# A hybrid conv/gMLP trunk: group A's LayerNorm placed between output products, four convolution operations per projection tile, late page splits, 1/rms chains on GpSimd

## The chip, the cores and the metric

One Trainium2 chip, one of its cores. The metric is the device time of one execution in microseconds (us); lower is better. The kernel before takes 972.72 us (median of 3 runs, 972.19 to 973.91). The engines are TensorE (PE; its weight loads are listed apart as PEld), VectorE (DVE), ScalarE (ACT), GpSimd (POOL) and SyncE (SP), which issues the DMAs here.

## The reference

There are two layers over 256 tokens of width 1024, in float32. Each layer is a half SwiGLU (1024 to 2816 to 1024), a mixer, and a second half SwiGLU; an RMSNorm stands ahead of each, and one at the end.

```
h = rms_norm(x, mix_norm[l]);  p = h @ w_in[l]        # split into A, B, C
a = silu(layer_norm(conv31(a_val * sigmoid(a_gate)) + conv_a_b))      # group A, 384 channels
b = gelu(b_u) * (tril(w_s) applied to layer_norm(gelu(b_v)) + b_s)    # group B, 256 channels
c = c_b * conv3(c_c * c_x)                                            # group C, 384 channels
x = x + concat(a, b, c) @ w_out[l]
x = x + 0.5 * (silu(h @ w_gate) * (h @ w_up)) @ w_down                # each half SwiGLU
```

## The kernel before

Activations lie with channels on partitions (128 x 256 tiles), except the residual `x_sb`, which lies with tokens on partitions in four banks (`c`: half of the tokens, `h`: half of the channels). Weights come as a stream of 128 x 1024 pages in the order of use, through 5 raw buffers (`load_to`, L137), loaded by the SP queue. Most pages are split into a rounded part `hi` (ACT, L151) and a rest `lo` (DVE, L152), so that TensorE can work with fast float32r products: `mm_wide` (L186) takes two, `mm_three` and `mm_out` (L202) three matmuls per block. The three `w_out` pages of group A are used unsplit (`native`, L155), by slow float32 matmuls (L206). `split_to` (L144) splits ahead of use, up to `AHEAD` pages and never beyond `state["cap"]`. Each `lo` is ordered behind the last operation of the latest 1/sqrt chain that the program had written before it (`held[0]`, set in `rsqrt`, L287).

The compiler's scheduler orders each engine's instructions: the earlier a statement stands in the program, the higher its priority, and an instruction that is not ready is passed by later ones. On the chip each engine then runs its list in order. `pin` (L97) fixes an instruction behind the one that the program wrote before it on the same engine. `mm_wide`, `mm_native`, transposes, sums and rows are pinned; `mm_three` and `mm_out` are not.

A half SwiGLU (`ffn`, L414) goes over 22 tiles f: gate and up products, an evacuation through DVE and ACT into the split `m2`, and the down products of tile f - 2 into four PSUM banks. The last three tiles' down products are taken bank by bank (`bank`), each bank is added to `x_sb`, squared and summed, and `Norm.turn` transposes it for the next stage, a bank later (`drain_banks`, L398). `Norm.rstd` then makes 1/rms by a chain of 12 small DVE operations (`rsqrt`, L270). `Norm.lead` (L384) starts the next stage: the first half (4 of 8 blocks) of three tiles, then the second halves; the matmuls that spread 1/rms over the partitions (`rows`, L375, `pb`, L299) stand behind the first tile's second half.

The very first norm has nothing before it: the first two pages are used natively, then `sums` (L343) squares the input, adds it up, and sums over channels on TensorE, with a 1/sqrt chain on DVE, and only then comes the first split page.

The mixer (`mixer`, L568) projects 19 tiles by `mm_three`. Three of them are made in `lead`; each of the 16 others draws `BACK` = 3 operations from the list of convolution steps of group A (`conv_ops`, L539): 21 per channel tile and 63 in all, each four ACT products with one DVE addition, or one DVE multiply-add, or one of two closing sums. 48 are drawn so; the remaining 15 follow after group B and C. Then `layer_norm` (L516) of group A is written: mean over channels on TensorE (L521), centring on DVE (L525), squares on ACT (L527), sums on TensorE (L309), the 1/sqrt chain on DVE, a row on TensorE (L299), scaling on DVE (L722), Silu on ACT (L724). The 20 output products of groups B and C (5 pages, 4 banks, 60 matmuls) are written behind it but are unpinned, so they run ahead of it. The 12 native output products of group A close the stage bank by bank.

Of the kernel before, what the change touches and what calls it, by code (L numbers as in the profile page):

```python
# [59 lines left out]
PARTS = 15  # L60
LOAD_AHEAD = 5
AHEAD = 11
PACE = 1.6
NEXT = 5
WORK = 12
# [3 lines left out]
LAST = 3  # L69
STEPS = 3  # L70
AFTER = 2
WIDE = 16
BACK = 3
# [3 lines left out]
def hybrid_trunk(ctx, tc, x_t, x_n, par, gain, w_st, b_s, wts, out):  # L77
# [124 lines left out]
    def mm_out(ps, x2, page, c, h, first, last):  # L202

        t, n = slice(c * P, (c + 1) * P), slice(h * N, (h + 1) * N)
        if len(x2.shape) == 2:
            nc.tensor.matmul(ps, x2[:, t], page[:, n], start=first, stop=last)  # L206
            return
        xh, xl = x2[:, 0, t], x2[:, 1, t]
        wh, wl = (p[:, n] for p in page)
        nc.tensor.matmul(ps, xh, wh, start=first, stop=False)  # L210
        nc.tensor.matmul(ps, xh, wl, start=False, stop=False)  # L211
        nc.tensor.matmul(ps, xl, wh, start=False, stop=last)  # L212
# [57 lines left out]
    def rsqrt(ss, scale, eps, name, n=TC):  # L270
# [5 lines left out]
        nc.vector.tensor_scalar(m, ss, scale, eps, ALU.mult, ALU.add)  # L276
        yi = t("i", dtype=I32)
        nc.vector.tensor_scalar(yi, m.bitcast(I32), -0.5, RSQRT_SEED, ALU.mult, ALU.add)
# [3 lines left out]
        nc.vector.tensor_mul(g, m, y)  # L282
        for it in range(3):
            r = t("r")
            y2 = t("y") if it < 2 else t("out", 4)
            nc.vector.scalar_tensor_tensor(r, g, -0.5, y, ALU.mult, ALU.mult)
            held[0] = nc.vector.scalar_tensor_tensor(y2, r, 1.5, y, ALU.add, ALU.mult)  # L287
            if it < 2:
                g2 = t("g")
                nc.vector.scalar_tensor_tensor(g2, r, 1.5, g, ALU.add, ALU.mult)  # L290
                g = g2
            y = y2
# [22 lines left out]
    class Norm:  # L315
# [54 lines left out]
        def rstd(self):  # L370
            s = tmp.tile([P, TC], F32, tag="rs_s", name=f"{self.id}_s")
            nc.vector.tensor_add(s, self.ss[:, :, 0], self.ss[:, :, 1])
            self.rs = rsqrt(s, 1.0 / D, RMS_EPS, self.id)
# [10 lines left out]
        def lead(self, tiles, want):  # L384

            ks = range(DT // 2), range(DT // 2, DT)
            got = None
            for mm, ps, w in tiles:
                mm(ps, w, self.act, ks[0])
                while self.later:  # L390
                    self.later.pop(0)()
            for mm, ps, w in tiles:
                mm(ps, w, self.act, ks[1])
                if got is None:
                    got = self.rows(want)
# [18 lines left out]
    def ffn(l, s, norm, nxt):  # L414
# [5 lines left out]
        if norm.first:  # L420
# [7 lines left out]
            norm.sums()  # L428
# [3 lines left out]
            rb, = norm.rows([AF.Copy])  # L432
# [7 lines left out]
        mm_wide(tiles[1][1], w1[1], act, range(DT))  # L440
        rh = tmp.tile([P, TC], F32, tag="rh", name=f"{nm}_rh")
# [74 lines left out]
    def layer_norm(tiles, eps, name, between=None, more=1):  # L516
# [13 lines left out]
        if between is not None:  # L530
            for _ in range(STEPS):
                between()
        y = rsqrt(token_sums(sq, name), 1.0 / (n * P), eps, name)
        if between is not None:
            for _ in range(more):
                between()
        return xc, row(y, name)
# [30 lines left out]
    def mixer(l, norm, nxt):  # L568
# [9 lines left out]
        state["cap"] = state["at"] + NIN + NB + NC  # L578
# [92 lines left out]
        xc, pr = layer_norm(vs, LN_EPS, f"{nm}_lv", step, AFTER)  # L671
# [43 lines left out]
        for k in range(NA, DT):  # L715
            split_mix(k)
        drain(len(back))
        use([MM], [MM, SM])
        xc, pr = layer_norm(conv, LN_EPS, f"{nm}_la")
        for i in range(NA):  # L720
# [5 lines left out]

        po = {b: ps_d.tile([P, N], F32, tag=f"d{b[0]}{b[1]}", name=f"{nm}_po{b[0]}{b[1]}")
              for b in banks}
        first, last = OUT_ORDER[0], OUT_ORDER[-1]
# [5 lines left out]
        state["cap"] = None  # L735
# [88 lines left out]
```

## Time and profile before

| | |
|---|---|
| median of 3 runs | 972.72 us |
| the profiled execution's own time | 972.09 us |
| its span, first to last instruction | 970.4 us |
| PE busy | 941.5 us (97%) |
| DVE busy | 703.9 us (73%) |
| ACT busy | 534.7 us (55%) |
| POOL busy | 2.3 us, 14 instructions |
| granted TensorE clock, mean | 0.987 |

Times inside the trace count from the start of the span. The granted clock has two levels, 2.4 GHz (1.00) and 1.2 GHz; a mean between them is a mixture over the stretch. TensorE is busy nearly all the time, so what can be won lies in its idle stretches and in the parts that ran at the lower clock.

### The profile page before, as it was taken

Reading aid. Unit: us, or ns where it says so; the run is one execution under the profiler, and the core shown is the slowest. Engines: PE = TensorE matmul, PEld = TensorE weight load, DVE = VectorE, ACT = ScalarE, POOL = GpSimd, SP = SyncE. Lnnn points to the kernel's source line nnn. Section 1 sums busy time; section 2 is a strip of 40 time slices with the busy share of each in tenths; the row PEclk is TensorE's granted clock in tenths of the full one; section 3 lists DMA queues with packets and bytes.
Section 4 is the critical chain, followed back from the end, with each engine's and each line's share of the span. In section 5 each row is a group of like instructions: output and inputs, shape, how many; then the busy total and the mean of one; then the engine's idle time right before and its main releaser. Section 6 shows DMA issues by size and latency. Waiting matters only on the chain.

```text
span 970.4 us, 13953 instructions
## 1 busy us (share of the span) xinstructions
PE 941.5 (97%) x5192; PEld 803.7 (83%) x5192; DVE 703.9 (73%) x1202; ACT 534.7 (55%) x906; POOL 2.3 (0%) x14
## 2 busy tenths in 40 slices
PE   7999999999989999999999999999999799999996
PEld 6888888889957888888878888888998488888884
DVE  5986666679978966666696666666898698666634
ACT  4865455468446755545565455455863576455512
POOL 0000000000000000000000000000000000000000
PEclk9999999999989999999999999999999799999999
DMA  8895555525117965555455555553430488555301
GB/s 290 314 321 192 184 195 185 185 88 174 61 43 239 328 213 194 187 185 193 153 191 183 191 195 183 187 194 111 157 127 1 136 293 290 193 195 192 113 1 43
DMA packets 48451, 172.22 MB, mean 177 GB/s; under 512 B 5376, under 2 KB 5760, under 8 KB 48384
## 3 DMA queue, kind: packets, MB, share of 16 engines
q1 hardware_dynamic: 48384, 171.34, 50.6%
q8 instruction: 40, 0.66, 0.3%
q14 instruction: 27, 0.22, 0.1%
HBM read 170.27 MB, written 1.05 MB: 177 GB/s over the span
## 4 chain that ended last, share of the span: by engine, by line
PE 88%; DVE 5%; DMA 3%; ACT 2%; issue 1%; SPq 0%; DVEq 0%; ACTq 0%
PE f_pu L191 15%; PE f_pg L191 15%; PE f_pd L210 8%; PE f_pd L211 8%; PE f_pd L212 8%; PE f_pu L192 8%; PE f_pg L192 8%; PE m_p L199 4%; PE m_p L200 4%; PE m_p L198 4%; DMA raw<-wts 3%; PE m_po L206 2%; DVE lo L152 1%; PE m_po L210 1%; PE m_po L211 1%
## 5 line engine op out<-in xcount | busy, mean ns | idle before, releaser
L152 DVE TENSOR_TENSOR lo<-raw,hi 128x1024 fp32r<-128x1024 f32 x310 | 377.2, 1223 | 185.2 <-ACT hi L151 168.3
L151 ACT CAST hi<-raw 128x1024 fp32r<-128x1024 f32 x310 | 323.8, 1049 | 258.3 <-PE f_pg L191 88.8
L191 PE MATMUL f_pg<-ffn_norm_x,hi 128*128 128x512 f32 x696 | 250.8, 400 | 1.4 <-DVE ffn_norm_x L368 1.4
L191 PE MATMUL f_pu<-ffn_norm_x,hi 128*128 128x512 f32 x696 | 250.8, 400 | 0.0
L192 PE MATMUL f_pg<-ffn_norm_x,lo 128*128 128x256 f32 x696 | 195.9, 281 | 0.0
L192 PE MATMUL f_pu<-ffn_norm_x,lo 128*128 128x256 f32 x696 | 195.4, 281 | 0.0
L191 PEld LDWEIGHTS f_pg<-ffn_norm_x,hi 128*128 128x128 f32 x696 | 131.5, 189 | 34.0 <-DVE ffn_norm_x L368 2.6
L191 PEld LDWEIGHTS f_pu<-ffn_norm_x,hi 128*128 128x128 f32 x696 | 130.8, 188 | 32.2
L210 PE MATMUL f_pd<-hi,f_m 128*128 128x512 f32 x352 | 138.9, 395 | 2.2 <-DVE f_wu_sm L221 2.2
L211 PE MATMUL f_pd<-lo,f_m 128*128 128x512 f32 x352 | 138.3, 393 | 0.0
L212 PE MATMUL f_pd<-hi,f_m 128*128 128x512 f32 x352 | 136.5, 390 | 0.0
L192 PEld LDWEIGHTS f_pg<-ffn_norm_x,lo 128*128 128x128 f32 x696 | 132.0, 190 | 3.0
L192 PEld LDWEIGHTS f_pu<-ffn_norm_x,lo 128*128 128x128 f32 x696 | 131.6, 189 | 0.0
L199 PE MATMUL m_p<-mix_norm_x,hi 128*128 128x256 f32 x304 | 86.8, 287 | 0.8 <-DVE mix_norm_x L368 0.8
L200 PE MATMUL m_p<-mix_norm_x,lo 128*128 128x256 f32 x304 | 85.9, 284 | 0.0
L198 PE MATMUL m_p<-mix_norm_x,hi 128*128 128x256 f32 x304 | 85.0, 286 | 0.0
L210 PEld LDWEIGHTS f_pd<-hi,f_m 128*128 128x128 f32 x352 | 66.1, 188 | 19.4 <-DVE f_wu_sm L221 3.4
L212 PEld LDWEIGHTS f_pd<-hi,f_m 128*128 128x128 f32 x352 | 66.0, 188 | 14.9 <-DVE f_m L467 0.7
L211 PEld LDWEIGHTS f_pd<-lo,f_m 128*128 128x128 f32 x352 | 66.1, 188 | 10.4
L199 PEld LDWEIGHTS m_p<-mix_norm_x,hi 128*128 128x128 f32 x304 | 58.2, 191 | 1.8 <-DVE mix_norm_x L368 1.2
L200 PEld LDWEIGHTS m_p<-mix_norm_x,lo 128*128 128x128 f32 x304 | 58.2, 192 | 0.2 <-issue 0.2
L198 PEld LDWEIGHTS m_p<-mix_norm_x,hi 128*128 128x128 f32 x304 | 57.3, 191 | 0.2 <-issue 0.2
(230 smaller groups left out, 821.5 us busy)
## 6 DMA issues: line engine op xcount, KB each, us to landing
raw<-wts SPq DMA_DIRECT2D x316, 512.0 KB, 4.3
xt<-x_t SPq DMA_DIRECT2D x4, 256.0 KB, 5.4
raw<-wts SPq DMA_DIRECT2D x4, 256.0 KB, 5.6
x_sb<-x_n SPq DMA_DIRECT2D x2, 512.0 KB, 7.2
out<-y SPq DMA_DIRECT2D x4, 256.0 KB, 2.2
wst<-w_st SPq DMA_DIRECT2D x2, 256.0 KB, 3.7
gfin<-gain SPq DMA_DIRECT2D x1, 512.0 KB, 5.6
bsb<-b_s SPq DMA_DIRECT2D x2, 128.0 KB, 3.8
```

The lines of the kernel that those rows point to most:

```text
L151: nc.scalar.copy(hi, loaded[i])
L152: after(nc.vector.tensor_sub(lo, loaded[i], hi), held[0])
L191: pin(nc.tensor.matmul(ps, wh, x2, start=k == 0, stop=False))
L192: pin(nc.tensor.matmul(ps[:, 0, :], wl, x2[:, 0, :], start=False, stop=k == DT - 1))
L198: nc.tensor.matmul(ps, wh, x2[:, 0, :], start=k == 0, stop=False)
L199: nc.tensor.matmul(ps, wh, x2[:, 1, :], start=False, stop=False)
L200: nc.tensor.matmul(ps, wl, x2[:, 0, :], start=False, stop=k == DT - 1)
L206: nc.tensor.matmul(ps, x2[:, t], page[:, n], start=first, stop=last)
L210: nc.tensor.matmul(ps, xh, wh, start=first, stop=False)
L211: nc.tensor.matmul(ps, xh, wl, start=False, stop=False)
L212: nc.tensor.matmul(ps, xl, wh, start=False, stop=last)
```

## The change

It pins the output products and writes group A's LayerNorm as a generator, resumed after the 6th, 11th and 16th of the 20 output products. `BACK` rises to 4, so that all 63 convolution steps are drawn with the projections. The cap on page splits falls by the three `w_out` pages of group C, which are split just ahead of their products. `Norm.rstd` moves to GpSimd (15 operations in place of 12). `lead` writes `rows` ahead of all second halves. In the first SwiGLU the first split page's gate product stands ahead of `sums`, and `rows` behind the up product. Sizes change with it.

```diff
-PARTS = 15
+PARTS = 16
-AHEAD = 11
+AHEAD = 13
-NEXT = 5
-WORK = 12
+NEXT = 4
+WORK = 10
+CHAIN = (5, 10, 15)
-BACK = 3
+BACK = 4
...
     def mm_out(ps, x2, page, c, h, first, last):
...
-            nc.tensor.matmul(ps, x2[:, t], page[:, n], start=first, stop=last)
+            pin(nc.tensor.matmul(ps, x2[:, t], page[:, n], start=first, stop=last))
...
-        nc.tensor.matmul(ps, xh, wh, start=first, stop=False)
-        nc.tensor.matmul(ps, xh, wl, start=False, stop=False)
-        nc.tensor.matmul(ps, xl, wh, start=False, stop=last)
+        pin(nc.tensor.matmul(ps, xh, wh, start=first, stop=False))
+        pin(nc.tensor.matmul(ps, xh, wl, start=False, stop=False))
+        pin(nc.tensor.matmul(ps, xl, wh, start=False, stop=last))
...
-    def rsqrt(ss, scale, eps, name, n=TC):
+    def rsqrt(ss, scale, eps, name, n=TC, eng=None):
+        v = nc.vector if eng is None else eng
...
-            nc.vector.scalar_tensor_tensor(r, g, -0.5, y, ALU.mult, ALU.mult)
-            held[0] = nc.vector.scalar_tensor_tensor(y2, r, 1.5, y, ALU.add, ALU.mult)
+            if eng is None:
+                v.scalar_tensor_tensor(r, g, -0.5, y, ALU.mult, ALU.mult)
+                held[0] = v.scalar_tensor_tensor(y2, r, 1.5, y, ALU.add, ALU.mult)
+            else:
+                v.tensor_mul(r, g, y)
+                v.tensor_scalar(r, r, -0.5, 1.5, ALU.mult, ALU.add)
+                v.tensor_mul(y2, r, y)
             if it < 2:
                 g2 = t("g")
-                nc.vector.scalar_tensor_tensor(g2, r, 1.5, g, ALU.add, ALU.mult)
+                if eng is None:
+                    v.scalar_tensor_tensor(g2, r, 1.5, g, ALU.add, ALU.mult)
+                else:
+                    v.tensor_mul(g2, r, g)
...
         def rstd(self):
-            nc.vector.tensor_add(s, self.ss[:, :, 0], self.ss[:, :, 1])
-            self.rs = rsqrt(s, 1.0 / D, RMS_EPS, self.id)
+            nc.gpsimd.tensor_add(s, self.ss[:, :, 0], self.ss[:, :, 1])
+            self.rs = rsqrt(s, 1.0 / D, RMS_EPS, self.id, eng=nc.gpsimd)
...
         def lead(self, tiles, want):
...
+            got = self.rows(want)
             for mm, ps, w in tiles:
                 mm(ps, w, self.act, ks[1])
-                if got is None:
-                    got = self.rows(want)
...
     def ffn(l, s, norm, nxt):
...
             split_to(4)
-            norm.sums()
             tiles[1] = [psum(wide, f"{nm}_1_pg")]
             w1 = weights(2, False)
             mm_wide(tiles[1][0], w1[0], act, range(DT))
-            rb, = norm.rows([AF.Copy])
+            norm.sums()
...
         mm_wide(tiles[1][1], w1[1], act, range(DT))
+        if norm.first:
+            rb, = norm.rows([AF.Copy])
...
     def mixer(l, norm, nxt):
...
-        state["cap"] = state["at"] + NIN + NB + NC
+        state["cap"] = state["at"] + NIN + NB
...
-        for k in range(NA, DT):
+        drain(len(back))
+        state["cap"] = None
+        use([MM], [MM, SM])
...
+        ln = layer_norm(conv, LN_EPS, f"{nm}_la")
+        xc = None
+        for n, k in enumerate(OUT_ORDER[:DT - NA]):
             split_mix(k)
-        drain(len(back))
-        use([MM], [MM, SM])
-        xc, pr = layer_norm(conv, LN_EPS, f"{nm}_la")
+            w = weights(1, False)[0]
+            for i, (c, h) in enumerate(banks):
+                mm_out(po[c, h], mix[k], w, c, h, k == first, k == last)
+                if n * len(banks) + i in CHAIN:
+                    xc = next(ln)
+        xc, pr = xc
...
-        for k in OUT_ORDER[:DT - NA]:
-            w = weights(1, False)[0]
-            for c, h in banks:
-                mm_out(po[c, h], mix[k], w, c, h, k == first, k == last)
```

The generator `layer_norm` stops three times: after mean, centring and squares; after sums and the 1/sqrt chain (on DVE, as before); after the row.

## Rows read from the trace of the kernel before

**Rows 1.** Waits of PE over the whole span: total us, times, longest.

```profile
PE m_po L206 <- ACT m_ay L724: 2.5, 1, 2.5
...
PE f_pg L191 <- DVE ffn_norm_x L368: 1.4, 2, 1.0
```

**Rows 2.** Stretches: length, busy time (count) per engine, clock, DMA share, GB/s.

```profile
264.05:299.32 35.27, 31.61 (x117) 20.83 (x116) 26.42 (x56) 17.35 (x31) 0.64 (x1) 0.90 0.23 81
737.12:773.64 36.52, 31.56 (x117) 21.00 (x115) 25.90 (x56) 17.61 (x33) 0.00 (x0) 0.86 0.20 68
...
218.00:264.00 46.00, 45.92 (x384) 44.97 (x383) 43.86 (x90) 30.98 (x62) 0.00 (x0) 1.00 0.34 115
```

**Rows 3.** Timeline of PE, first mixer's output stage: start, duration, instruction, wait before it.

```profile
277.18 0.39 PE L210 MATMUL m_po<-hi,m_mix 128*128 128x512 f32 x1
...
277.86 0.39 PE L210 MATMUL m_po<-hi,m_mix 128*128 128x512 f32 x1
...
283.71 1.23 PE L299 MATMUL m_la_pb<-ident,m_la_out 128*128 128x128 f32 x4 [1.96 <-DVE m_la_out L287]
286.08 7.37 PE L206 MATMUL m_po<-raw,m_ao 128*128 128x512 f32 x12 [1.15 <-ACT m_ao L724]
293.29 0.60 PE L362 MATMUL ffn_norm_pt<-ident,x_sb 128*128 128x128 f32 x4
293.72 2.74 PE L206 MATMUL m_po<-raw,m_ao 128*128 128x512 f32 x6
```

**Rows 4.** Timelines of ACT and DVE there: a page's hi, the 1/sqrt chain, its lo.

```profile
272.55 1.03 ACT L151 CAST hi<-raw 128x1024 fp32r<-128x1024 f32 x1
...
281.78 0.16 DVE L276 TENSOR_SCALAR m_la_m<-m_la_ps 128x2 f32<-128x2 f32 x1 [1.67 <-PE m_la_ps L309]
...
283.57 1.23 DVE L152 TENSOR_TENSOR lo<-raw,hi 128x1024 fp32r<-128x1024 f32 x1
```

**Rows 5.** Groups of DVE, 264.05 to 279.45, then 210 to 264.05: busy, mean ns.

```profile
L563 DVE SCALAR_TENSOR_TENSOR m_ac_acc<-apad,par_sb,m_ac_acc 128x256 f32<-128x256 f32 x10 | 4.3, 478 | 0.1
L556 DVE TENSOR_TENSOR m_ac_acc<-m_ac_acc,m_ac_t 128x1024 f32<-128x1024 f32 x2 | 2.5, 1226 | 1.3 <-ACT m_ac_t L554 1.2
...
L152 DVE TENSOR_TENSOR lo<-raw,hi 128x1024 fp32r<-128x1024 f32 x12 | 14.4, 1216 | 0.5 <-ACT hi L151 0.5
```

**Rows 6.** Timeline of PE around the first norm.

```profile
19.28 0.58 PE L309 MATMUL ffn_norm_ps<-ones,ffn_norm_sq 128*128 128x1 f32 x4 [3.88 <-DVE ffn_norm_sq L351]
...
24.52 0.48 PE L191 MATMUL f_pu<-ffn_norm_x,hi 128*128 128x512 f32 x1
...
27.38 0.39 PE L191 MATMUL f_pg<-ffn_norm_x,hi 128*128 128x512 f32 x1
```

**Rows 7.** Timeline of PE at the end of the first and the last SwiGLU.

```profile
193.49 0.40 PE L210 MATMUL f_pd<-hi,f_m 128*128 128x512 f32 x1
...
196.69 0.42 PE L210 MATMUL f_pd<-hi,f_m 128*128 128x512 f32 x1
...
952.56 0.40 PE L210 MATMUL f_pd<-hi,f_m 128*128 128x512 f32 x1
...
954.60 0.50 PE L210 MATMUL f_pd<-hi,f_m 128*128 128x512 f32 x1
```

**Rows 8.** Timelines: POOL's rows, DVE beside one, ACT and PE after the first mixer.

```profile
1.10 0.17 POOL L253 MEMSET zpad<- 128x2 f32 x3
1.29 0.29 POOL masks.py:199 TENSOR_SCALAR_AFFINE_SELECT ident<-ident 128x128 f32<-128x128 f32 x1
72.47 0.74 POOL L260 TENSOR_SCALAR_AFFINE_SELECT wst<-wst 128x512 f32<-128x512 f32 x1 [70.88 <-DMA wst<-w_st]
...
72.64 0.85 DVE L467 TENSOR_TENSOR f_m<-f_m,f_m 128x256 fp32r<-128x256 f32 x1
...
300.94 0.19 ACT L356 ACTIVATION_READ_ACCUMULATOR ffn_norm_sq<-x_sb 128x1 f32 x1
...
303.12 0.40 PE L191 MATMUL f_pg<-ffn_norm_x,hi 128*128 128x512 f32 x1
```

More of the change, by code (lines that the diff above doesn't have):

```diff
@@ L275, in rsqrt @@
         m = t("m")
-        nc.vector.tensor_scalar(m, ss, scale, eps, ALU.mult, ALU.add)
+        v.tensor_scalar(m, ss, scale, eps, ALU.mult, ALU.add)
         yi = t("i", dtype=I32)
-        nc.vector.tensor_scalar(yi, m.bitcast(I32), -0.5, RSQRT_SEED, ALU.mult, ALU.add)
+        v.tensor_scalar(yi, m.bitcast(I32), -0.5, RSQRT_SEED, ALU.mult, ALU.add)
         y = yi.bitcast(F32)
         g = t("g")
-        nc.vector.tensor_mul(g, m, y)
+        v.tensor_mul(g, m, y)
         for it in range(3):
@@ L386, in lead @@
             ks = range(DT // 2), range(DT // 2, DT)
-            got = None
             for mm, ps, w in tiles:
@@ L513, in finish, with layer_norm @@
                 nc.sync.dma_start(out[c, :, h * N:(h + 1) * N], y)
-    def layer_norm(tiles, eps, name, between=None, more=1):
+    def layer_norm(tiles, eps, name, eng=None):
         n = len(tiles)
@@ L529, in layer_norm @@
             sq.append(q)
[L530 to L537, printed above, removed]
+        yield
+        y = rsqrt(token_sums(sq, name), 1.0 / (n * P), eps, name, eng=eng)
+        yield
+        yield xc, row(y, name)
     def conv_ops(l, i, ap, out, name):
@@ L670, in mixer @@
         step()
-        xc, pr = layer_norm(vs, LN_EPS, f"{nm}_lv", step, AFTER)
+        ln = layer_norm(vs, LN_EPS, f"{nm}_lv")
+        for n in (STEPS, AFTER):
+            next(ln)
+            for _ in range(n):
+                step()
+        xc, pr = next(ln)
         vn = []
@@ L712, in mixer @@
             pass
-        for k in range(NA, DT):
-            split_mix(k)
-        drain(len(back))
-        use([MM], [MM, SM])
-        xc, pr = layer_norm(conv, LN_EPS, f"{nm}_la")
+        drain(len(back))
+        state["cap"] = None
+        use([MM], [MM, SM])
+        po = {b: ps_d.tile([P, N], F32, tag=f"d{b[0]}{b[1]}", name=f"{nm}_po{b[0]}{b[1]}")
+              for b in banks}
+        first, last = OUT_ORDER[0], OUT_ORDER[-1]
+        ln = layer_norm(conv, LN_EPS, f"{nm}_la")
+        xc = None
+        for n, k in enumerate(OUT_ORDER[:DT - NA]):
+            split_mix(k)
+            w = weights(1, False)[0]
[4 more added lines that the diff above has]
+        xc, pr = xc
         for i in range(NA):
@@ L725, in mixer @@
             mix[i] = a
-        po = {b: ps_d.tile([P, N], F32, tag=f"d{b[0]}{b[1]}", name=f"{nm}_po{b[0]}{b[1]}")
-              for b in banks}
-        first, last = OUT_ORDER[0], OUT_ORDER[-1]
-        for k in OUT_ORDER[:DT - NA]:
-            w = weights(1, False)[0]
-            for c, h in banks:
-                mm_out(po[c, h], mix[k], w, c, h, k == first, k == last)
         wn = dict(zip(OUT_ORDER[DT - NA:], native(NA)))
-        state["cap"] = None
         split_to(state["at"] + NEXT)
```

## The prediction

> **What bounds the kernel.** The table of busy times gives TensorE 97% of the span, so the next question is where its remaining idle time lies. The list of its waits names the stages: group A's LayerNorm at the end of each mixer, and the evacuation of the transposed residual ahead of a SwiGLU [rows 1]. In the view by stretches, the output stage of the two mixers lasts 35.27 and 36.52 us with 31.61 and 31.56 us busy, at a mean clock of 0.90 and 0.86, while in the projections ahead of it TensorE leaves nothing idle and VectorE is busy 43.86 of 46.00 us [rows 2]. So the output stages lose time twice, by idling and at the lower clock, and the projection stage has hardly any VectorE time to give.
>
> The timeline of the first output stage shows how. The 60 matmuls of groups B and C run at 0.68 us a product (277.18 to 277.86). Then TensorE waits for one link of LayerNorm after another, and the clock falls: the row's four records take 1.23 us against 0.60 for four such records later, and the first 12 native records take 7.37 us where 6 take 2.74, thus 1.89 too long [rows 3]. Idle 3.66, native 1.89 and row 0.63 make 6.2 us in layer 0; idle 4.96 and the same clock losses make 7.5 in layer 1. The ceiling of this part is 13.7 us.
>
> **The change part by part**, in us against the profiled execution's 972.09; the median of the runs shown is 972.72, so 0.6 is added at the end.
>
> *LayerNorm between products.* The mean follows product 6, the sums product 11, the row product 16, and 4 products (2.7) cover scaling and Silu. That hides the chain if convolution is finished by product 6, and gives up to -13.7. Two new waits come in its place.
>
> First, the splits on use. Before, a page's hi stood ready from 272.55 + 1.03 on, but its lo ran only at 283.57, straight behind the chain that began at 281.78: each lo is ordered behind the latest chain written before it [rows 4]. In the changed program the first C page is split before the chain is written, the second and third behind it. Count from the first product: 11 products are 7.5, the mean inside them about 1, the sums about 1.2 (estimates from the records' starts), the chain 1.8 [rows 4], the lo 1.2, in all 12.7 to 12.9; the 13th product is reached at 10.4, can run its first matmul, and waits for lo: about 2.4 per mixer. It is nothing if the sums come early, and at most the chain and the lo, 3.0. I take 2.4, as both of its links stand in rows.
>
> Second, convolution moves into the projections. 10 multiply-adds (4.3) and 2 additions (2.5) ran behind 264.05, besides the closing sums [rows 5]; they now stand ahead of the output products' operands on VectorE. Against that, three lo leave the projections (3 x 1.22 [rows 5]), PARTS and AHEAD let about one more be made earlier (1.2), and 2.1 were idle [rows 2]: 6.8 + 1.1 for the closing sums - 7.0 is about 1 us by which the first product starts late. Pinning matters here: the products can no longer go out of order around a missing rest of an operand. Bounds: 0, when all of the slack is usable, and 5, when neither the idle time nor the earlier page helps; I take 1, from the balance. The scalar work on ACT has 15 us free in the same stretch [rows 2] and costs nothing; if ACT were late, the additions behind it would be. The three loads are the same, only their raw buffers are held longer, and the SP queue then brings the next stage's pages later; the 12 native products (about 11 us) cover that, and if not, the next SwiGLU would wait for a page.
>
> Sum for both mixers: -13.7 + 2 x (2.4 + 1.0) = -6.9.
>
> *First norm.* TensorE waited 3.88 us until 19.28 for the squares, then ran the gate product at the lower clock until the row; the up product began at 24.52, the next tile at 27.38, so a page's product is 2.86 at full clock [rows 6]. Now the gate product fills the hole from 15.4 to 18.2, the sums come at 19.28 as before, the up product runs until 22.6, and the row behind it finds its chain done. The next tile needs a PSUM buffer that VectorE frees some 1.5 us after the row: 24.5 instead of 27.38, **-2.9**. Bounds: -4 if that buffer is free at once, -1 if VectorE's page splits stand ahead of it.
>
> *Pinned products at the ends of the SwiGLUs.* At present 14 matmuls of other banks (193.49 to 196.69) fill the time until the last tile's operand is there; at the last SwiGLU it is there after 2.04 (952.56 to 954.60) [rows 7]. Pinned, the first bank offers 6 matmuls, 1.36 us, as filler. So 0.7 to 1.8 are lost at three ends and 0.6 at the fourth; with 1.2, in all +4.2. The first banks are then done earlier relative to the rest, so the waits for the transposed residual (1.4 [rows 1]) should go: **+2.8**, between +0.7 and +6.
>
> *Chains on GpSimd.* At five stage changes the chain becomes 15 dependent GpSimd operations, and the row, pinned, now stands ahead of all second halves. Time allowed in the one after the first mixer: the squares are there at 301.13, the third first half begins at 303.12 and takes 1.4, so 3.4 us [rows 8]. No such operation is in the trace: fills of 128x2 take 0.17 for three, the select of 128x128 takes 0.29, one of 128x512 takes 0.74 [rows 8]; VectorE's 11-step chain takes 1.8 [rows 4]. Bounds per step are 0.06 and 0.74, so 1 to 11 us per chain; I take 0.20, between the nearest rows, so 3.0. One thing speaks for more: while GpSimd ran its select, a VectorE subtraction that takes 0.42 elsewhere took 0.85 [rows 8], so the two hold each other up. One operation of 0.7 in the way makes 3.7, which is 0.3 late, with the hand-overs 0.4; five times: **+2.0**, bounds 0 and +38. If TensorE comes late here, tile evacuations wait for the row too.
>
> By itself, what a page says of this: the Trainium skill, "SBUF — State Buffer", section "SBUF: two separate sides", has VectorE and GpSimd share one port pair as an exclusive lock, held for a whole instruction, also against VectorE operations with two SBUF inputs. The subtraction above agrees. By that rule every lo that falls into a chain adds its whole length to it, which is the first rival's mechanism.
>
> *Sizes.* WORK falls to 10 and NEXT to 4; four pages are what the next stage's lead uses, and no row shows a wait for a work buffer: 0, and the next stage's splits would be late if it is short.
>
> Sum: -6.9 - 2.9 + 2.8 + 2.0 = -5.0, so 967.1 in a profiled execution and **967.7** as a median.
>
> **The rivals.** *GpSimd chains decide* (slower). Place: the row ahead of the second halves, five times. If VectorE's operations with two inputs stand in the chain's way, say two of 0.7 and two lo of 1.2 (3.8), a chain takes 6.8, TensorE is 3.4 late each time, 17 in all instead of 2: 967.7 + 15 = **982.7**. It decides when a chain is 1.4 late, that is from 4.8 us on, as all other parts are worth 7.0. For it: the stretched subtraction, and that splits are no longer ordered behind these chains, so they may fall into them. Against: in the mixers' lead the scheduler can pass the row with unpinned matmuls.
>
> *VectorE bounds the projections* (no change). If the output products start 4 late instead of 1, the mixers give -0.9 and the total is +1.0: **973.7**. For it: 43.86 of 46.00 busy. Against: the moved splits free as much as convolution adds.
>
> *Clean overlap.* Neither new wait nor late chains: -13.7 - 2.9 + 2.8 = -13.8, so **958.9**.
>
> That the change doesn't do what it says has no place of its own: if convolution ends after product 6, the fixed places turn into waits, which is the second rival.
>
> **How the numbers follow.** Forecast 0.44, clean overlap 0.20, GpSimd 0.20, VectorE 0.16. A difference of 0.2%, 1.9 us, is about what a measurement of this kernel can tell from none. Faster: clean 0.20, forecast 0.38 (its bounds reach past 970.8 for the rest), VectorE 0.02, so 0.60. Same: VectorE 0.12, forecast 0.05, GpSimd 0.03, so 0.20. Slower: 0.20. The range runs from the clean case to where most of the GpSimd case is left out: 958 to 979.
>
> **What would show it.** In the changed profile the waits of TensorE for m_la_out and m_ay should be gone, the native records should take 2.74 for 6 from the start, and a wait for lo of about 2.4 should stand before the 13th product. The wait for the first squares should be near 1 us, and a wait for the split m2 should stand at each SwiGLU's end. POOL should have 75 operations more, with each row waiting for them by under 1 us. Waits of several us for the GpSimd result, or output products starting 4 us behind the last projection, would make the prediction wrong.

## The result and the profile after

The changed kernel takes 1016.82 us (median of 4 runs, 1013.92 to 1025.95) against 972.46 (971.61 to 973.91) for the kernel before: 1.0471 times, with an interval of 1.0403 to 1.0538. The prediction was 967.7, faster. The changed kernel's four runs spread over 12 us, the slowest at the lowest mean clock (0.961) and the fastest at the highest (0.977), where the kernel before spreads over 2.3; the profiled run, used in this section, is the slowest of them.

From the page of the changed kernel: the table of busy times and TensorE's rows of the 40 slices.

```profile
span 1024.2 us, 14005 instructions
PE 964.9 (94%) x5192; PEld 823.6 (80%) x5192; DVE 695.1 (68%) x1142; ACT 532.1 (52%) x906; POOL 21.1 (2%) x89
...
PE   7899999989897999999989999999898989999996
...
PEclk9899999989978999999989999999898989999999
```

Apart from GpSimd (21.1 us, 2.3 before) no other engine is fuller than before: VectorE is at 695.1 us (703.9 before). TensorE's idle time is 59.3 us (1024.2 - 964.9) against 28.9 before, 30.4 more. Its busy time is 23.4 more (964.9 - 941.5) for the same arithmetic. So more than two fifths of the loss is matmuls that take longer. The slices show where: apart from the two ends of the run, both rows fall to 8 or 7 around the stage changes and stay at 9 between them.

TensorE's waits over the whole span (us in total, times, longest) answer to [rows 1]:

```profile
PE ffn_norm_pb L310 <- POOL ffn_norm_out L295: 9.3, 3, 3.4
PE f_pd L211 <- ACT f_m L476: 6.9, 4, 2.1
PE mix_norm_pb L310 <- POOL mix_norm_out L295: 6.5, 2, 3.3
PE m_po L211 <- DVE m_co L667: 4.8, 1, 4.8
PE f_pg L192 <- DVE ffn_norm_x L379: 4.4, 5, 1.0
PE m_po L211 <- DVE m_cv L667: 4.3, 1, 4.3
PE m_po L212 <- DVE lo L153: 4.1, 2, 2.1
PE f_pd L211 <- DVE f_wu_sm L222: 3.3, 1, 3.3
PE f_pg L192 <- DVE f_g L470: 2.4, 1, 2.4
...
PE ffn_norm_ps L320 <- DVE ffn_norm_sq L362: 0.9, 1, 0.9
```

The waits for group A's LayerNorm are gone, as intended, and the wait for the first squares fell from 3.9 to 0.9. In their place stand stops of 2 to 5 us at fourteen places (of the rows above: five for the GpSimd result, three of four for f_m, two each for the first output product and lo, one each for f_wu_sm and f_g). What a stop does to the matmuls behind it is seen in TensorE's timeline of the changed kernel, at the end of the first SwiGLU and in the first output stage [rows 3, 7]:

```profile
197.96 0.39 PE L213 MATMUL f_pd<-hi,f_m 128*128 128x512 f32 x1
200.47 0.50 PE L211 MATMUL f_pd<-hi,f_m 128*128 128x512 f32 x1 [2.13 <-ACT f_m L476]
...
276.93 0.28 PE L201 MATMUL m_p<-mix_norm_x,lo 128*128 128x256 f32 x1
281.99 0.77 PE L211 MATMUL m_po<-hi,m_mix 128*128 128x512 f32 x1 [4.79 <-DVE m_co L667]
282.56 0.63 PE L212 MATMUL m_po<-lo,m_mix 128*128 128x512 f32 x1
...
287.13 0.39 PE L212 MATMUL m_po<-lo,m_mix 128*128 128x512 f32 x1
...
297.52 0.80 PE L212 MATMUL m_po<-lo,m_mix 128*128 128x512 f32 x1 [2.05 <-DVE lo L153]
```

A record that takes 0.39 ahead of a stop takes 0.63 behind it, until some 4 to 5 us later. The view by stretches gives the clock of three of these, behind the stop at the SwiGLU's end, the one for the first output product and the one for the first mixer's row (length, busy and count of PE, PEld, DVE, ACT, POOL, then clock, DMA share, GB/s):

```profile
200.47:204.93 4.46, 4.46 (x13) 3.38 (x14) 1.16 (x2) 0.72 (x2) 0.00 (x0) 0.62 0.29 103
281.99:288.28 6.29, 6.29 (x18) 4.97 (x19) 1.66 (x3) 0.00 (x0) 0.00 (x0) 0.65 0.25 86
219.40:222.00 2.60, 2.60 (x12) 2.60 (x13) 0.00 (x0) 1.32 (x3) 0.00 (x0) 0.50 0.00 0
```

0.50 is the level of 1.2 GHz throughout. The prediction counted the new stops at their length alone.

The GpSimd chain of the first mixer's lead, from the timeline of POOL (first and last row of the chain's 15, the stretched one and the row ahead of it):

```profile
214.36 0.19 POOL L383 TENSOR_TENSOR mix_norm_s<-mix_norm_ss 128x2 f32<-128x2 f32 x1 [131.72 <-ACT mix_norm_sq L367]
...
214.92 0.19 POOL L281 TENSOR_SCALAR mix_norm_i<-mix_norm_m 128x2 int32<-128x2 int32 x1
215.19 1.04 POOL L285 TENSOR_TENSOR mix_norm_g<-mix_norm_m,mix_norm_i 128x2 f32<-128x2 f32 x1
...
219.15 0.20 POOL L295 TENSOR_TENSOR mix_norm_out<-mix_norm_r,mix_norm_y 128x2 f32<-128x2 f32 x1
```

One operation takes 0.19, and one that needs its result starts 0.28 behind it. The fourth took 1.04, beside a page's rest on VectorE that ran from 214.96 for 1.22. The whole chain takes 4.99; the other four take 4.23, 5.00, 4.99 and 4.68, each with a stretched operation in it.

The time that TensorE can bridge is the other half of such a wait. After the first mixer, in order of time: the last page's rest on VectorE ahead of the chain's start, ACT's last square, TensorE's last record ahead of the row, and the row.

```profile
322.11 1.23 DVE L153 TENSOR_TENSOR lo<-raw,hi 128x1024 fp32r<-128x1024 f32 x1
...
322.51 0.19 ACT L367 ACTIVATION_READ_ACCUMULATOR ffn_norm_sq<-x_sb 128x1 f32 x1
...
323.35 0.28 PE L193 MATMUL f_pg<-ffn_norm_x,lo 128*128 128x256 f32 x1
327.06 0.94 PE L310 MATMUL ffn_norm_pb<-ident,ffn_norm_out 128*128 128x128 f32 x4 [3.43 <-POOL ffn_norm_out L295]
```

From the squares on, which are there at 322.70, TensorE has 0.9 us of work left, until 323.63; the prediction allowed 3.4. The chain starts at 322.78, 11.3 us behind the start of the second of the four additions into the residual (311.46). In the kernel before that was 7.7 (293.49 to 301.16), with one page's rest in between; here there are four.

### The profile page after: what moved, and what is told of

The parts are those of the page before. It is cut to its first block, busy times and chain, and to the rows that moved or that the text cites. A ratio compares the mean times of both kernels' runs of the same rounds, so it can differ in the third digit from the quotient of the medians.

```text
span 1024.2 us, 14005 instructions
## 1 busy us (share of the span) xinstructions
PE 964.9 (94%) x5192; PEld 823.6 (80%) x5192; DVE 695.1 (68%) x1142; ACT 532.1 (52%) x906; POOL 21.1 (2%) x89
## 4 chain that ended last, share of the span: by engine, by line
PE 75%; issue 16%; DVE 3%; DMA 2%; POOL 2%; ACT 2%; SPq 0%; POOLq 0%; DVEq 0%; ACTq 0%
PE f_pu L192 16%; PE f_pg L192 15%; PE f_pd L211 8%; PE f_pu L193 8%; PE f_pg L193 8%; PE f_pd L212 8%; PE f_pd L213 8%; DMA raw<-wts 2%; PE m_p L199 2%; PE m_p L200 2%; PE m_p L201 2%; ACT hi L152 1%; DVE lo L153 1%; ACT mix_norm_sq L367 0%; DMA wst<-w_st 0%
## 5 line engine op out<-in xcount | busy, mean ns | idle before, releaser
L192 PE MATMUL f_pu<-ffn_norm_x,hi 128*128 128x512 f32 x696 | 253.4, 403 | 0.0
L211 PE MATMUL f_pd<-hi,f_m 128*128 128x512 f32 x352 | 141.8, 403 | 10.2 <-ACT f_m L476 6.9
L212 PE MATMUL f_pd<-lo,f_m 128*128 128x512 f32 x352 | 140.8, 400 | 0.0
L213 PE MATMUL f_pd<-hi,f_m 128*128 128x512 f32 x352 | 140.2, 398 | 0.0
L211 PEld LDWEIGHTS f_pd<-hi,f_m 128*128 128x128 f32 x352 | 67.5, 192 | 27.7 <-ACT f_m L476 8.6
L200 PE MATMUL m_p<-mix_norm_x,hi 128*128 128x256 f32 x304 | 88.1, 291 | 0.7 <-DVE mix_norm_x L379 0.7
L201 PE MATMUL m_p<-mix_norm_x,lo 128*128 128x256 f32 x304 | 88.1, 291 | 0.0
L199 PE MATMUL m_p<-mix_norm_x,hi 128*128 128x256 f32 x304 | 87.3, 294 | 0.0
L213 PEld LDWEIGHTS f_pd<-hi,f_m 128*128 128x128 f32 x352 | 67.7, 192 | 15.7 <-DVE f_m L477 0.6
L200 PEld LDWEIGHTS m_p<-mix_norm_x,hi 128*128 128x128 f32 x304 | 60.3, 198 | 1.5 <-DVE mix_norm_x L379 1.1
L199 PEld LDWEIGHTS m_p<-mix_norm_x,hi 128*128 128x128 f32 x304 | 59.6, 200 | 0.4 <-issue 0.3
```

The source lines that it names most:

```text
L192: pin(nc.tensor.matmul(ps, wh, x2, start=k == 0, stop=False))
L199: nc.tensor.matmul(ps, wh, x2[:, 0, :], start=k == 0, stop=False)
L200: nc.tensor.matmul(ps, wh, x2[:, 1, :], start=False, stop=False)
L201: nc.tensor.matmul(ps, wl, x2[:, 0, :], start=False, stop=k == DT - 1)
L211: pin(nc.tensor.matmul(ps, xh, wh, start=first, stop=False))
L212: pin(nc.tensor.matmul(ps, xh, wl, start=False, stop=False))
```

## The experiments

The runs fall into three sets: one part undone in the changed kernel; all suspected costs out, and one put back; the GpSimd chain alone in the kernel before. Each was timed beside the kernel before, so differences below are differences of the ratios times 972.5 us. The changed kernel's 1.0471 is +45.8 by this measure, and its interval is 6.6 us wide to either side; that holds for every difference taken against it.

### One part undone in the changed kernel

**Chains on VectorE.**

```diff
-            nc.gpsimd.tensor_add(s, self.ss[:, :, 0], self.ss[:, :, 1])
-            self.rs = rsqrt(s, 1.0 / D, RMS_EPS, self.id, eng=nc.gpsimd)
+            nc.vector.tensor_add(s, self.ss[:, :, 0], self.ss[:, :, 1])
+            self.rs = rsqrt(s, 1.0 / D, RMS_EPS, self.id)
```

> The changed kernel with its five 1/rms chains on VectorE again (12 operations in place of 15); the row stays ahead of all second halves. Theory G (the engine of the chain is the cost): the five waits of TensorE for norm_out, 15.8 us together in the changed kernel's profile, and the lower clock behind each of them go, about 4 us at each of five places, so about 20 us less than the changed kernel: about 997 us. Theory R (the early place of the row is the cost, whatever engine makes the chain): VectorE's list is full there too, so the waits stay above 1.5 us each and the time falls by less than 6 us: above 1010 us.

Measured: 990.79 us, 1.0184 (1.0168 to 1.0199), 27.9 less. Of 15.8 us of waits for the row one remains, in its list of waits:

```profile
PE ffn_norm_pb L310 <- DVE ffn_norm_out L291: 0.5, 1, 0.5
```

Theory G holds against R: the row's early place costs little when the chain runs on VectorE. But this edit brings back more than the engine. A chain on VectorE sets `held[0]` again, so page splits are ordered behind it as before, and the 27.9 are for both together.

**SwiGLU products free.**

```diff
-            mm_out(pd[c, h], mid[f], wd[f], c, h, f == 0, f == FT - 1)
+            mm_out(pd[c, h], mid[f], wd[f], c, h, f == 0, f == FT - 1, lambda i: i)
```

(`mm_out` takes `pin` as a last argument.)

> The changed kernel with the SwiGLUs' down products unpinned (the mixers' output products stay pinned). Theory F (too little filler): the waits of 2.1, 2.1, 2.1 and 0.5 us for the last tile's split operand go, and the lower clock that follows each of the first three (12 records in 4.6 us where 2.8 is normal) with them: 3 x (2.1 + 1.8) + 0.5, about 12 us less, about 1005 us. Theory B (the time comes back as waits for the transposed residual at the start of the next stage, since the first bank is then done later): the gain is under 6 us, above 1011 us.

Measured: 1008.5 us, 1.0373 (1.0353 to 1.0392), 9.5 less. The waits for the last tile's operand are gone, and those for the GpSimd row rose from 15.8 to 16.9, those for the residual's split from 5.1 to 5.8. The stop of 3.3 us for f_wu_sm is gone too, which neither theory had counted. Between the theories, nearer to F; the second set gives the clean size.

**The last projection in another bank.**

```diff
+            if j == IN_ORDER[-1]:
+                use([MM], state["sm"])
             ps = psum([P, T], f"{nm}_p{j}")
```

> The changed kernel with the mixer's last projection in a PSUM buffer of the three ps_mm ones; in the changed kernel it lies in the bank that the first output product writes. Theory P (the bank decides the late start): the waits of 4.8 and 4.3 us of the first output product for VectorE's read of that bank fall below 1.5 us, and the lower clock behind them goes (18 records in 6.5 us where 4.1 is normal): 2 x (3.3 to 4.8 + 2.4), 11 to 14 us less, about 1004 us. Theory V (VectorE is that late with everything, the second rival of the prediction): the wait moves to the mean, the operand or the sums in the same stage, and less than 4 us are won: above 1012 us.

Measured: 1006.76 us, 1.0357 (1.0334 to 1.0379), 11.1 less. Neither 4.8 nor 4.3 remains; instead the first product's third matmul waits 0.9 in each mixer for its operand's rest. Theory P holds.

**First norm as before.**

```diff
             split_to(4)
+            norm.sums()
...
-            norm.sums()
+            rb, = norm.rows([AF.Copy])
...
-        if norm.first:
-            rb, = norm.rows([AF.Copy])
```

> The changed kernel with the first norm in the order of the kernel before (sums ahead of the first split page's gate product, row behind it). The prediction's step (the new order wins 2.9 us): the time rises by 3 us. Theory D (the first down product waits for an evacuation that stands behind page splits that wait for their loads, and those loads come no sooner; the clock then falls): what the new order wins by the first tiles is given back, and the end of the first SwiGLU's fourth tile comes within 1 us of where it was or earlier: the time stays within 3 us or falls by up to 4 us. Read first by when TensorE begins tile 3: 36.89 us in the kernel before, 39.77 in the changed one.

Measured: 1020.62 us, 1.0488 (1.0471 to 1.0506), within the changed kernel's interval. Tile 3 begins at 37.53 instead of 39.77, so the new order loses there, but the total does not show it. Inconclusive; it was taken up again below.

### All suspected costs out, and one put back

**Only the LayerNorm's placement left.** The four edits above, and two more:

```diff
-            got = self.rows(want)
             for mm, ps, w in tiles:
                 mm(ps, w, self.act, ks[1])
+                if got is None:
+                    got = self.rows(want)
...
-        xc = None
+        xc, h0 = None, held[0]
         for n, k in enumerate(OUT_ORDER[:DT - NA]):
             split_mix(k)
+            h1, held[0] = held[0], h0
             w = weights(1, False)[0]
+            held[0] = h1
```

> The changed kernel with all suspected costs taken out together: chains on VectorE, row behind the first tile's second half, SwiGLU products unpinned, first norm in the order before, the mixer's last projection out of the first output bank, and the splits of group C's last two pages no longer ordered behind the LayerNorm chain. What stays is the LayerNorm between output products, with four convolution operations per tile. Main theory (those six are the whole loss, and the placement itself wins): with only the bank moved, layer 0's output stage lasted 34.81 us from the first output product (272.77) to the next stage's first product (307.58), against 35.71 before (264.05 to 299.76); 2.06 of it was the wait for lo. So about 3 us per mixer less than the kernel before: about 966 us, 962 to 969. Rival C (convolution in the projections costs what the placement wins): 971 to 975 us.

Measured: 960.99 us, 0.9885 (0.9867 to 0.9904), 11.2 less than the kernel before and better than expected. TensorE's timeline of the first output stage, and its stretch:

```profile
263.80 0.50 PE L211 MATMUL m_po<-hi,m_mix 128*128 128x512 f32 x1
...
265.42 0.50 PE L213 MATMUL m_po<-hi,m_mix 128*128 128x512 f32 x1 [0.89 <-DVE m_mix L627]
265.76 0.39 PE L211 MATMUL m_po<-hi,m_mix 128*128 128x512 f32 x1
...
279.00 0.60 PE L310 MATMUL m_la_pb<-ident,m_la_out 128*128 128x128 f32 x4
```

```profile
263.80:293.90 30.10, 29.20 (x119) 19.73 (x119) 22.20 (x47) 16.52 (x28) 0.64 (x1) 1.00 0.43 145
```

The stage lasts 30.10 us at full clock, 35.71 before; the row waits for nothing and takes 0.60 (1.23 in [rows 3]). The other mixer's stage went from 36.96 (737.12 to 774.08) to 31.12 (732.03 to 763.15). Together -11.4, as much as the profiled executions differ (972.09 and 960.69). This version beats both kernels.

**New first norm in it** (the changed kernel's order put back, against the run above):

```diff
-            norm.sums()
...
-            rb, = norm.rows([AF.Copy])
+            norm.sums()
...
+        if norm.first:
+            rb, = norm.rows([AF.Copy])
```

> The first kernel of this set with the change's order of the first norm (gate product ahead of the sums, row behind the up product). Alone it tells what that order is worth without other stops. The prediction's step: 2.9 us less than the first of this set. Theory D (first evacuations behind page splits, 2.4 and 3.3 us waits and a lower clock): tile 3 began at 39.77 us with the new order and at 37.53 with the old one in two profiles with the rest of the change: 2.2 us more than the first of this set.

Measured: 960.38 us, 0.9874 (0.9852 to 0.9895). The interval overlaps that of the run above, so no difference can be told. Tile 3's up product begins at 38.20 (38.99 above). The wait for squares fell to 1.6, but a new one took its place, in the list of waits:

```profile
PE f_pg L192 <- DVE f_g L472: 2.4, 1, 2.4
```

Neither theory's number came. With the down products free, the 3.3 us stop and the low clock behind it do not occur, so that stop needs the new order and the pinning together (with the pinning and the old order it was 0.5).

**Early row in it** (against the run of 960.99 us, as are the next three):

```diff
+            got = self.rows(want)
             for mm, ps, w in tiles:
                 mm(ps, w, self.act, ks[1])
-                if got is None:
-                    got = self.rows(want)
```

> The first kernel of this set with the row ahead of all second halves, the chain on VectorE. With the chain on VectorE the changed kernel's waits for it were 0.5 us in all, so Theory G: within 2 us of the first of this set. Theory R (an early row costs by itself): 3 us or more above it.

Measured: 962.62 us, 0.9901 (0.9884 to 0.9917), +1.6, with overlapping intervals. Theory G.

**Pinned SwiGLU products in it.**

```diff
-            mm_out(pd[c, h], mid[f], wd[f], c, h, f == 0, f == FT - 1, lambda i: i)
+            mm_out(pd[c, h], mid[f], wd[f], c, h, f == 0, f == FT - 1)
```

> The kernel of 961.0 us (LayerNorm placed, six costs taken out) with the SwiGLUs' down products pinned again, as in the change. Theory F (too little filler before the last tile's operand): three waits of 2.1 us and one of 0.5, each of the three with a lower clock behind it; alone in the changed kernel their removal was worth 8.3 us: 967 to 972 us. Theory B (what was seen there came from the long chains around the same stage change): less than 4 us, under 965 us.

Measured: 975.0 us, 1.0020 (1.0003 to 1.0037): +13.1, more than either theory. Its list of waits shows a second place:

```profile
PE f_pd L211 <- ACT f_m L477: 6.9, 4, 2.1
PE f_pd L211 <- DVE f_wu_sm L222: 4.8, 3, 2.4
...
PE f_pg L192 <- DVE ffn_norm_x L379: 0.6, 2, 0.3
```

The 6.9 are the ends. The 4.8 (1.1 without pins) are at the starts: tile 1's up product lies in bank `d00`, the first down product needs that bank, and pinned it cannot let the other three banks go first. That is read from the list and the program; no run moved this bank.

**lo behind the chain in it.**

```diff
-            h1, held[0] = held[0], h0
...
-            held[0] = h1
```

> The kernel of 961.0 us with the rest (lo) of group C's last two pages ordered behind the LayerNorm chain again, as in the change. Theory H (the hold is the wait): TensorE waits 2.06 us in each mixer for lo, and the clock falls behind it: 2 x (2.1 to 3.5), so 965 to 968 us. Theory V (VectorE comes to those splits no earlier without the hold): within 1.5 us of it.

Measured: 968.33 us, 0.9937 (0.9916 to 0.9957), +5.1. Theory H: in its list of waits,

```profile
PE m_po L212 <- DVE lo L153: 4.1, 2, 2.1
```

**Shared bank in it.**

```diff
-            if j == IN_ORDER[-1]:
-                use([MM], state["sm"])
```

> The kernel of 961.0 us with the mixer's last projection in the first output product's bank again, as in the change. Theory P: the first output products wait 4.8 and 4.3 us for VectorE's read of that bank, and the clock falls behind it; in the changed kernel the move was worth 10 us, so 969 to 975 us. Theory V (without long chains ahead of it VectorE reads the bank earlier): less than 4 us.

Measured: 972.2 us, 0.9989 (0.9980 to 0.9999), +10.1. Theory P: in its list of waits,

```profile
PE m_po L211 <- DVE m_co L668: 5.1, 1, 5.1
PE m_po L211 <- DVE m_cv L668: 4.7, 1, 4.7
```

The sum closes. From -11.2: pins 13.1, bank 10.1, lo 5.1, row 1.6 and first norm -1.1 make +17.6. The changed kernel with its chains on VectorE has all of these and measured +17.9. Each term is known to some 2 to 3 us, so that it closes to 0.3 is partly luck. The 27.9 for the chains are the step from there to the changed kernel's +45.8.

### The GpSimd chain alone, in the kernel before

**Chains on GpSimd.** The change's own edit of `rsqrt` and `rstd`, nothing else:

```diff
-            self.rs = rsqrt(s, 1.0 / D, RMS_EPS, self.id)
+            self.rs = rsqrt(s, 1.0 / D, RMS_EPS, self.id, eng=nc.gpsimd)
```

> The kernel before with nothing changed but the five 1/rms chains on GpSimd; the row still stands behind the first tile's second half. The chain takes 4.1 to 5.0 us there in the changed kernel's profile against 1.8 on VectorE, so it is 2.3 to 3.2 later. Theory G (engine alone is enough): the row waits about 1 us or more at the SwiGLUs' leads, where the products are pinned, and the clock falls behind it: 6 to 16 us more, about 982 us. Theory GR (only engine and early row together cost): the second half of one tile, 1.4 us, and the free order of the mixers' lead cover the rest: within 3 us of the kernel before, under 975.5 us.

Measured: 989.56 us, 1.0174 (1.0153 to 1.0195), +16.9: more than Theory G's range, and the row itself waits only 1.6 in all. TensorE waits 14.1 us for the residual's split (`ffn_norm_x`), 1.4 in [rows 1]. VectorE's timeline after the first mixer shows what held it:

```profile
305.95 1.22 DVE L152 TENSOR_TENSOR lo<-raw,hi 128x1024 fp32r<-128x1024 f32 x1
310.87 0.17 DVE L452 TENSOR_SCALAR f_rh<-ffn_norm_out 128x2 f32<-128x2 f32 x1 [3.70 <-POOL ffn_norm_out L294]
310.95 1.23 DVE L152 TENSOR_TENSOR lo<-raw,hi 128x1024 fp32r<-128x1024 f32 x1
312.09 0.69 DVE L378 TENSOR_TENSOR ffn_norm_x<-ffn_norm_xg,ffn_norm_x 128x512 fp32r<-128x512 f32 x1
```

VectorE stands 3.70 us at the first operation that reads the chain's result, with the residual's last split behind it. The chain also starts late, 10.7 us behind the second addition into the residual (7.7 before).

**That reader on GpSimd too.**

```diff
-        nc.vector.tensor_scalar(rh, norm.rs, 0.5, None, ALU.mult)
+        nc.gpsimd.tensor_scalar(rh, norm.rs, 0.5, None, ALU.mult)
```

> The kernel before with the five chains on GpSimd, as in the run that took 989.6 us, and also the one small operation that halves the chain's result for the SwiGLU's end (rh, 128x2) on GpSimd. In that run VectorE stood still for 3.70 us at that operation after the first mixer, with the last split of the transposed residual and two page splits behind it in its list, and TensorE's waits for that split were 14.1 us against 1.4 before. Theory Q (VectorE's queue behind the reader of the chain is the cost): those waits fall to about 2 us and the lower clock behind them goes: 973 to 978 us. Theory L (the longer chain is the cost by itself): the wait moves to the row or to the first evacuation, and the time stays above 984 us.

Measured: 991.93 us, 1.0184 (1.0169 to 1.0199). Theory Q fell as to the time: VectorE no longer stands, works on page splits, and the chain pays for it, in POOL's timeline:

```profile
305.62 1.19 POOL L278 TENSOR_SCALAR ffn_norm_m<-ffn_norm_s 128x2 f32<-128x2 f32 x1
306.89 1.05 POOL L280 TENSOR_SCALAR ffn_norm_i<-ffn_norm_m 128x2 int32<-128x2 int32 x1
...
311.33 1.27 POOL L292 TENSOR_TENSOR ffn_norm_r<-ffn_norm_g,ffn_norm_y 128x2 f32<-128x2 f32 x1
...
313.95 0.20 POOL L294 TENSOR_TENSOR ffn_norm_out<-ffn_norm_r,ffn_norm_y 128x2 f32<-128x2 f32 x1
```

From 305.34 to 314.15 it takes 8.8 us (the chain after the second mixer 8.7, the others 4.7 to 5.3), and the row waits up to 4.0.

**Chains on VectorE, without the order on page splits.** On GpSimd the chain no longer sets `held[0]`, so two things change with the engine. This run takes the second alone:

```diff
+            h0 = held[0]
             self.rs = rsqrt(s, 1.0 / D, RMS_EPS, self.id)
+            held[0] = h0
```

> The kernel before with its five chains on VectorE as they are, but page splits no longer ordered behind them (the order behind the LayerNorms' and the first norm's chain stays). Theory H (the order is what keeps page splits, 1.22 us each, out of VectorE's list while the transposed residual is made; with the chains on GpSimd it fell away, and three of them ran between 300.6 and 307.2): a good part of the 17.2 us is here: TensorE's waits for the split residual rise from 1.4 to 5 us or more, 978 to 988 us. Theory E (the engine of the chain is the cost, the order is worth nothing): within 2 us of the kernel before.

Measured: 991.59 us, 1.0188 (1.0158 to 1.0218), +18.3 with no chain on GpSimd. Theory H. VectorE's timeline after the first mixer shows six page rests among the twelve steps of the chain:

```profile
304.05 0.16 DVE L276 TENSOR_SCALAR ffn_norm_m<-ffn_norm_s 128x2 f32<-128x2 f32 x1
304.12 1.22 DVE L152 TENSOR_TENSOR lo<-raw,hi 128x1024 fp32r<-128x1024 f32 x1
305.25 0.16 DVE L278 TENSOR_SCALAR ffn_norm_i<-ffn_norm_m 128x2 int32<-128x2 int32 x1
305.32 1.22 DVE L152 TENSOR_TENSOR lo<-raw,hi 128x1024 fp32r<-128x1024 f32 x1
...
312.61 0.15 DVE L287 SCALAR_TENSOR_TENSOR ffn_norm_out<-ffn_norm_r,ffn_norm_y 128x2 f32<-128x2 f32 x1
```

The chain lasts from 303.37 to 312.76, 9.4 us; before, from 301.16 to 304.66 with no page's rest in it. It also starts later, 10.2 us behind the second addition into the residual (7.7 before).

**Order put back through a VectorE copy.**

```diff
+            seen = tmp.tile([P, TC], F32, tag="rs_seen", name=f"{self.id}_seen")
+            held[0] = nc.vector.tensor_copy(seen, self.rs)
```

> The kernel before with the five chains on GpSimd and the order put back: page splits written later stand behind a small VectorE copy (128x2) of each chain's result. Theory H: no page split falls into the chain, so it takes about 4.1 us and starts as early as before (301.16 where it was 305.99 without the order); the row is then about 1 us later than before: 973 to 978 us. Theory E (engine alone): VectorE stands at the copy until the chain ends and the splits behind it come late in its place: 985 us or more.

Measured: 992.68 us, 1.0199 (1.0180 to 1.0218). Theory E's number, though Theory H's half on the chain came true. It is short again (304.94 to 309.24), and it starts 7.7 us behind the second addition into the residual, as before. (The 301.16 and 305.99 of the expectation also hold what earlier stages had lost.) But VectorE stands at the copy:

```profile
309.27 0.17 DVE L385 COPY ffn_norm_seen<-ffn_norm_out 128x2 f32<-128x2 f32 x1 [2.58 <-POOL ffn_norm_out L294]
...
310.55 0.68 DVE L378 TENSOR_TENSOR ffn_norm_x<-ffn_norm_xg,ffn_norm_x 128x512 fp32r<-128x512 f32 x1
```

**Order behind the residual's last addition, no reader on VectorE** (with `rh` on GpSimd).

```diff
+                add = nc.vector.tensor_add(x[c, h], ps, x[c, h])
...
         nxt.rstd()
+        held[0] = add
```

> The kernel before with chains and rh on GpSimd, so that no VectorE operation of the stage change waits for the chain, and page splits written later ordered behind the last addition into the residual, which VectorE does without waiting for GpSimd. Theory H (order and queue are the cost, GpSimd itself is harmless): the residual's splits come in time and the chain ends by 310 us: under 980 us. Theory X (with GpSimd idle in VectorE's way or not, page splits then run beside the chain and stretch its operations from 0.2 to about 1.1 us each, as in the run with rh moved, where the chain took 8.9 us): above 985 us.

Measured: 988.36 us, 1.0166 (1.0149 to 1.0183). Theory X: the chain runs from 303.11 to 312.02, 8.9 us, though it starts 7.7 us behind the second addition as before, and the row waits up to 3.4. With the chain on GpSimd, either VectorE stands and holds up the residual's splits, or it works and stretches the chain; in four forms it cost 16.1 to 19.4 us. A form in which page splits keep off the chain while no VectorE operation waits for it was not tried.

## Why the prediction was wrong, step by step

Both signs that the prediction named against itself came: waits of several us for the GpSimd result, and output products that start over 4 us late.

| step | predicted | measured |
|---|---|---|
| LayerNorm between products | -13.7 | -11.2 |
| lo behind the chain | +4.8 | +5.1 |
| late start of output products | +2.0 | +10.1 |
| first norm | -2.9 | -1.1, not told from 0 |
| pinned SwiGLU products | +2.8 | +13.1 |
| chains on GpSimd | +2.0 | +27.9, early row +1.6 apart |

**LayerNorm's placement and the held lo were right**, mechanism and size: the waits for it are gone, the native records run at full clock, and the wait before the 13th product was 2.05 us (2.4 predicted). That 4.8 and 5.1 agree is partly luck: the two waits are 4.1, and the lower clock behind them, which the step left out, brings the rest. Of the 13.7, 1.8 went into two waits for the first operand's rest.

**The late start was mis-sized by its mechanism.** The step balanced VectorE's work and found it 1 us late. VectorE in fact reads the last projection 4.5 us behind the first output product's start, also where nothing is lost (268.32 against 263.80 in the run of 960.99 us). That lag matters only because of the bank: the last projection lies in `d00`, which the first output product writes. The prediction noted that pinned products cannot go around a missing operand, but not that they cannot go around an occupied bank. Its second rival saw a start 4 us late, with VectorE as the cause; moving one tile removed it with VectorE's work unchanged.

**Pinned SwiGLU products**: the step took 1.2 us lost at three ends, and 2.1 were. It had no term for the starts (4.8 us of waits in the clean kernel), which have the same bank `d00`. The saving on waits for the residual came about as predicted, 2.2 to 0.6. In the profiled executions (972.29 and 960.69) idle time grew by 9.8 us and busy time by 1.8; what the rest of the 13.1 is stays open.

**The chains failed worst**, in two terms of the step. One is the time allowed. The step read 3.4 us at one stage change of the kernel before; in the changed kernel TensorE ran out of work 0.9 to 2.1 us after the chain's start. The other is the chain, 3.0 and 3.7 with one operation in the way; it took 4.2 to 5.0. The 0.20 us per operation was right (0.19), but operations that depend on each other start 0.28 apart, and one or two in each chain were stretched. So TensorE was 2.9 to 3.4 late at each of five places, not 0.4, and all five add up to the 15.8 us of waits. In the run with the chains back on VectorE, and so with the order on page splits back, a chain took 2.5 to 3.5 and TensorE had work for 2.2 to 3.7. By these differences some 9 us of the 15.8 come from the longer chain and some 6 from the shorter time, nearly half of these after the first mixer.

Part of the missing time was never there: the step read one place, and even with the order back three of the five had 2.2 to 2.6. The rest comes from the order, to which the step gave no price: the prediction mentions only in a rival that page splits are no longer held behind these chains. After the first mixer the chain started 7.7 us behind the second addition into the residual in every run that held page splits back, on either engine, and 10.2 to 11.8 in those that did not. By the run without it, that order is worth 18.3 us in the kernel before on its own. How much of the 27.9 it makes is not separated, as no run has the changed kernel without the order and with its chains on VectorE.

The first rival named a stretched chain and put its turning point at 4.8 us; at a chance of 0.20 it was the right case. Its 3.4 us of lateness came, but it had reckoned them from a chain of 6.8 and 3.4 allowed, so that number is partly luck.

By itself, on the rule that the prediction weighed: the Trainium skill, "SBUF — State Buffer", section "SBUF: two separate sides", has a VectorE operation with two SBUF inputs hold the port pair that it shares with GpSimd for its whole length. The traces agree: in the chains shown, GpSimd operations of 0.19 became 1.04 to 1.27 beside page rests of 1.22.

**What no step priced** is the clock behind a stop: TensorE's busy time rose by 23.4 us, against 30.4 of idle time. In the kernel of 960.99 us it is 937.2, less than before. The prediction had read this loss in the old output stage [rows 3] and counted its return there, and then priced every new stop at its length. The loss has no fixed share: with the pinned SwiGLU products put back, 9.8 us more of idle time came with 1.8 of busy time.

Not settled: what the new sizes, the fourth convolution step per tile and the late page splits do apart (they stayed in all versions of the second set, so the -11.2 is for the placement with them), and the first norm's order, whose runs differ by less than their intervals.

## What to carry to other kernels

Before fixing an order by hand, list for each fixed instruction not only the operands but the PSUM bank that it writes and who must have read it: an out-of-order schedule had walked around both. A chain that is moved to another engine leaves behind the order that hung on it, so look for what was tied to it, and work out again how much time the chain has, at each of its places. Price a stop of a busy TensorE at its length, and expect a loss behind it for the lower clock: here between a fifth and four fifths of the length (1.8 to 9.8 with the pinned SwiGLU products, 23.4 to 30.4 in the changed kernel). Test the parts of a bundle one by one: the other parts of this one hid one that was worth 11 us.

## What the hardware showed unexpectedly

- Behind stops of 2 to 5 us TensorE mostly ran at 0.50 to 0.65 of its clock for some 4 us, in which a matmul of 128x512 took 0.63 us instead of 0.39 and started 0.43 behind the last instead of 0.23. Behind the 0.89 us waits of the run of 960.99 us it stayed at 0.39. It is not every stop: behind a wait of 2.13 us at 481 us in the run with pinned SwiGLU products, 12 records took 3.01.
- Two GpSimd operations in a row that do not depend on each other start 0.15 us apart (218.18 and 218.33), two that do 0.28.
